# A streaming encoder step: PSUM reuse by tile, single banks in the down projection, frames split in two parts

## The chip, the core and the metric

The kernel runs on one core of one Trainium2 chip. The metric is device time in microseconds (us). TensorE (PE) does the matmuls and transposes and writes PSUM, which has eight banks of 128 x 512 floats; VectorE (DVE) and ScalarE (ACT) read PSUM and SBUF; GpSimd (POOL) adds in SBUF and issues some DMAs; SyncE (SP) and ACT issue the other DMAs.

## What is computed

One step of a one-layer encoder for 1152 rows (1024 prompt frames and 8 x 16 sample frames) of width 1024. The part that the change touches is the end of memory attention, the norm after it and the feed-forward block:

```python
def _rmsnorm(x, g):
    xf = x.astype(jnp.float32)
    y = xf * lax.rsqrt(jnp.mean(xf * xf, axis=-1, keepdims=True) + EPS)
    return (y * g.astype(jnp.float32)).astype(x.dtype)

def _swiglu(h, w_gate, w_up, w_down):          # hidden width 2816
    return (jax.nn.silu(h @ w_gate) * (h @ w_up)) @ w_down

x = x + _merge(a_out, sb_out, g_out_sgu[l], g_out_sb[l], w_out[l])     # gMLP group and stick-breaking attention
x = x + _mem_attend(_rmsnorm(x, ln_mem[l]), mk, mv, w_mq[l], w_mo[l])  # ends in o @ w_mo, the out-projection
x = x + _swiglu(_rmsnorm(x, ln_ffn[l]), w_ffn_gate[l], w_ffn_up[l], w_ffn_down[l])
y = _rmsnorm(x, ln_final)
```

## The kernel before

Every float32 product is made from three matmuls: each operand is split into a high part (a cast on ACT) and a low part (the rest, a subtraction on DVE; `split`, L126 and L127), and `mm3` (L130 to L132) multiplies high by high, high by low and low by high. The rows go in nine tiles of 128. Python writes the work in one order, and a scheduler that knows estimated costs sets the order of each engine's queue from it; at run time each queue is strictly in order, and an instruction waits on semaphores for what it reads and for the last users of the buffer that it writes.

The last 920 us have three stages.

**Out-projection, 881 to 997 us** (`out_in`, `out_mm`, `turn_halves`). For each row tile `out_in` loads and splits the attention output `oh`, `ol`; `out_mm` makes two halves of 512 columns in the two banks of one PSUM pair tile `pp` and DVE adds each to the residual `xt` (L1013), which goes to `x2_d` by a POOL DMA (L1014). `norm` squares and sums the row on ACT (L148), takes the inverse root on POOL (`inv_rms`, L141 and L142) and scales on DVE (L150) into `xs`. `turn_halves` of the tile before transposes `xs` by eight small matmuls (L1025), four into each bank of another pair, and makes the right-hand operands of the feed-forward block: splits into `b11`, `b21`, `b22`, and the differences `t1` (L1031, L1032), `t2` (L1035), `t3` (two operations, L1042, on DVE) and `t4` (two operations, L1044, on POOL).

**Gate and up products, 997 to 1503 us.** A two-by-two block scheme makes each block product from seven instead of eight: 22 units (11 groups of hidden columns for gate and up), seven products each, 24 matmuls of 128 x 288 columns per product (`multiply`, L1154). The left operands come from `left`: weights loaded as `raw`, four sums on POOL (L1078), a cast on ACT and a subtraction on DVE into a weight tile `wg`. Four buffers of the pool `wr` and one of `w2` serve in turn, so five weight tiles are in the ring, and `refill(4)` keeps four ready ahead. The right operands are `b11`, `b21`, `b22` and the split frames `c5` to `c4`, which `frames(n)` makes from `t1` to `t4` in four calls of `split`, 128 x 576 each. The first unit begins while the last row tile has not been transposed: `multiply(1)` and `multiply(2)` stand ahead of the last `turn_halves`. Products go out of PSUM by ACT copies and DVE or POOL additions (L1144) and by `hid_d`, a DRAM buffer.

**Down projection, 1503 to 1791 us.** The 22 hidden groups go in six chunks, the first of two groups, the others of four. `load` fetches a group's `hid_d` rows (`hr`) and down weights (`raw`) on SP's queue, `prep` splits them (`hid`, `wd`). For each chunk and row tile a pair of banks takes the two halves, and DVE adds each half into the residual `xr` (L1280). The `xr` tiles come back from `x2_d` by nine POOL DMAs at the stage's start (L1251). In the last chunk the final norm follows each tile.

Two things set what waits. A PSUM tile is one unit of the dependency tracking: a pair tile holds two banks, and a matmul into one of them waits for users of the tile. When a pool is closed and another takes its space, the new pool's tiles wait for the users of the old pool; with `reuse_waits="tile"`, which the SBUF pools have here already, a new tile waits only for the users of the tiles that lay under it, and without it for every user of the pool. The PSUM pools were without it.

Of the kernel before, what the change touches and what calls it, by code (L numbers as in the profile page):

```python
# [9 lines left out]
F32 = mybir.dt.float32  # L10
F32R = mybir.dt.float32r
# [5 lines left out]
P = 128  # L17
D = 1024
KC = D // P
NT = 9  # L20
# [17 lines left out]
def stream_step(ctx: ExitStack, tc: tile.TileContext, I, O, cst):  # L38
    nc = tc.nc

    def pool(stack, name, bufs=1, **kw):
        return stack.enter_context(tc.tile_pool(name=name, bufs=bufs, reuse_waits="tile", **kw))

    const = ctx.enter_context(tc.tile_pool(name="const", bufs=1))
    stP = ctx.enter_context(ExitStack())
    psum = [stP.enter_context(tc.tile_pool(name="psum", bufs=1, space=PSUM))]
    small = ctx.enter_context(tc.tile_pool(name="small", bufs=8))
    dram = ctx.enter_context(tc.tile_pool(name="scratch", bufs=1, space=DRAM))

# [3 lines left out]
    def nm(s):  # L53
        uid[0] += 1
        return f"{s}_{uid[0]}"
# [915 lines left out]

    with ExitStack() as stE:
        stP.close()
        psum[0] = stE.enter_context(tc.tile_pool(name="psum_pairs", bufs=1, space=PSUM))
        stN, stS, stG = ExitStack(), ExitStack(), ExitStack()
        slots = pool(stE, "f_h", bufs=10)

        def slot(shape, name):
            return slots.tile(shape, F32R, tag="h", name=name)
# [36 lines left out]
        def turn_halves(xs, i):  # L1016
# [16 lines left out]
            if n0 < P:  # L1033
                new = both[:, 1, :, n0:P]
                nc.vector.tensor_tensor(out=t2[:, :, c1], in0=new, in1=t1[:, :, c1], op=sub)  # L1035
                split(b22[0][:, :, c1], b22[1][:, :, c1], new)
                for out, b, eng in ((t3, b11, nc.vector), (t4, b21, nc.gpsimd)):
                    t = out[:, :, c1]
                    for m in range(2):
                        x, y = t if m else t2[:, :, c1], b[m][:, :, c1].bitcast(F32)  # L1040
                        if out is t3:
                            eng.tensor_tensor(out=t, in0=x, in1=y, op=sub)  # L1042
                        else:
                            eng.tensor_tensor(out=t, in0=y, in1=x, op=ALU.add if m else sub)  # L1044
# [9 lines left out]
        stW.close()  # L1054

        cp = pool(stG, "g_c", side="right")
        w2 = pool(stG, "g_w", bufs=1, side="right")
        sp = pool(stG, "g_s", side="right")
        vp = [pool(stG, "g_p", side="right")]
        right = {1: b11, 2: b21, 3: b22}  # L1060
# [5 lines left out]
        def left(w, f, order):  # L1066
# [13 lines left out]
            for n in order:  # L1080
                if n in (3, 5) and not s:
                    sum_(5, a21, a22, ALU.add)
                    sum_(6, s[5], a11, ALU.subtract)
                    sum_(7, a11, a21, ALU.subtract)
                    sum_(3, a12, s[6], ALU.subtract)
                src = {1: a11, 2: a12, 4: a22}.get(n, s.get(n))
                pl = wr if count[0] % 5 else w2
                count[0] += 1
                hl = pl.tile([P, 2, 4, P], F32R, tag="w", name=nm("wg"))
                split(hl[:, 0], hl[:, 1], src)  # L1090
                yield n, hl

        def frames(n):

            hi = cp.tile([P, 4, TH], F32R, name=f"c{n}h")
            lo = cp.tile([P, 4, TH], F32R, name="c5l") if n == 5 else slot([P, 4, TH], f"c{n}l")
            for c in range(4):
                split(hi[:, c], lo[:, c], {5: t1, 6: t2, 7: t3, 4: t4}[n][:, c])
            right[n] = hi, lo

        def bank_pair():
            n = count[1] % 4
# [59 lines left out]

        def load(f):

            hr = []
            for g in range(2):
                t = xp[0].tile([P, TH], F32, tag="x", name=nm("hr"))
                nc.sync.dma_start(t, hid_d[f, :, g * TH:(g + 1) * TH])
                hr.append(t)
# [17 lines left out]
        for u in range(len(units)):  # L1187
# [3 lines left out]
            end = u == len(units) - 1  # L1191
            for k, n in enumerate(order_of(u)):
                if u == 0 and k == 0:
                    refill(3)
                    part[1] = vt("p1", 2)
                    nc.scalar.copy(part[1], multiply(1))
                    part[2] = multiply(2)
                    turn_halves(norm(npool, ins[-1][1], gffn), NT - 1)
                    stN.close()
                    vp.append(pool(stG, "g_v", side="right"))  # L1200
                    xp.append(pool(stE, "g_x", bufs=6))
                    frames(5)
                    continue
                if u == 0 and k == 1:
                    continue
                refill(4)
                if u == 0 and n in (3, 5, 6):
                    frames({3: 6, 5: 7, 6: 4}[n])
                acc = multiply(n)
                if n in (1, 5):  # L1210
                    part[n] = vt(f"p{n}", 2 if n == 1 else 1)
# [30 lines left out]
                    have.append(prep(*loads[k - 4]))  # L1242
        stG.close()

        xpool = pool(stE, "h_x", side="right")
        jp = pool(stE, "h_j", bufs=2, side="right")
        gfin = xpool.tile([P, D], F32, name="gfin")
        xr = []
        for i in range(NT):
# [16 lines left out]
        for c, fs in enumerate(chunks):  # L1266
# [72 lines left out]
```

## Time and profile before

| | before |
|---|---|
| median of 3 runs | 1804.79 us (1803.49 to 1807.76) |
| the profiled execution | 1804.37 us, span 1801.5 us |
| PE busy | 1729.4 us (96%) |
| DVE busy | 980.3 us (54%) |
| ACT busy | 675.8 us (38%) |
| POOL busy | 445.5 us (25%) |
| mean granted TensorE clock | 0.983 of full speed |

The span is the time from the first to the last instruction on the chip; some 3 us lie around it. PE is the engine that sets the end: what matters is where it idles and where its clock is at half. In the rows below, "[4.76 <-DVE xs L150]" behind a PE instruction says that PE was idle for 4.76 us before it and that the end of DVE's instruction of line 150, which wrote `xs`, released it. Pitch is the distance from one matmul's start to the next one's.

### The profile page before, as it was taken

How to read it: one execution, taken by the hardware profiler on the slowest of the kernel's cores; microseconds unless marked ns; L12 is line 12 of the kernel's file. 1: busy time of each engine (PE TensorE's matmuls, PEld its weight loads, DVE VectorE, ACT ScalarE, POOL GpSimd, SP SyncE). 2: the span in 40 equal slices, each digit the busy share in tenths (PEclk: the TensorE clock that was granted, in tenths of full speed). 3: DMA queues.
4: the chain of work that ended last, by engine and by line, in shares of the span. 5: the costliest groups of instructions: out<-in, count | busy, mean ns of one | idle time of the engine just before them, and what ended most of it. 6: DMA issues, size and time to landing. Idle time of an engine off the chain costs nothing.

```text
span 1801.5 us, 26249 instructions
## 1 busy us (share of the span) xinstructions
PE 1729.4 (96%) x10039; PEld 1500.7 (83%) x10039; DVE 980.3 (54%) x1471; ACT 675.8 (38%) x1326; POOL 445.5 (25%) x582
## 2 busy tenths in 40 slices
PE   8999998999999999999799799999999998999997
PEld 6889886777777799898687699999999997777775
DVE  5322336888778745546446754455444456344444
ACT  5322134766555435546321432333222332011123
POOL 1101223444333210000013444444444431000002
PEclk9999999999999999999899899999999999999999
DMA  8457135467544524435543132222222227122202
GB/s 284 147 199 247 64 128 186 147 204 243 166 118 133 191 95 132 129 121 173 161 129 106 35 100 88 76 79 78 74 74 74 74 74 279 50 100 100 99 8 98
DMA packets 175069, 227.93 MB, mean 127 GB/s; under 512 B 12064, under 2 KB 122272, under 8 KB 174944
## 3 DMA queue, kind: packets, MB, share of 16 engines
q1 hardware_dynamic: 143248, 161.89, 29.4%
q10 hardware_dynamic: 23504, 35.79, 5.4%
q0 software_dynamic: 8192, 28.58, 4.3%
q8 instruction: 79, 1.29, 0.3%
q14 instruction: 46, 0.38, 0.1%
HBM read 161.86 MB, written 64.36 MB: 126 GB/s over the span
## 4 chain that ended last, share of the span: by engine, by line
PE 65%; DVE 4%; issue 2%; DMA 2%; POOL 2%; ACT 2%; POOLq 0%; ACTq 0%; SPq 0%; DVEq 0%
PE pp L1154 27%; PE pp L130 6%; PE pp L131 6%; PE pp L132 6%; PE acc L385 3%; PE acc L130 2%; PE acc L131 2%; PE acc L132 2%; PE z L385 2%; PE tr L389 2%; PE av L385 1%; DMA raw<-in_cache_mem_v_dram 1%; PE ov L943 1%; PE ss L926 1%; DMA or<-oT_d 1%
## 5 line engine op out<-in xcount | busy, mean ns | idle before, releaser
L1154 PE MATMUL pp<-b,wg 128*128 128x288 f32 x1584 | 224.1, 298 | 4.8 <-ACT b L126 3.4
L1154 PEld LDWEIGHTS pp<-b,wg 128*128 128x128 f32 x1584 | 216.1, 190 | 5.9 <-ACT b L126 3.8
L130 PE MATMUL pp<-wd,hid 128*128 128x512 f32 x396 | 153.7, 404 | 8.2 <-DVE xr L1280 6.6
L131 PE MATMUL pp<-wd,hid 128*128 128x512 f32 x396 | 155.3, 394 | 0.0
L132 PE MATMUL pp<-wd,hid 128*128 128x512 f32 x396 | 153.1, 392 | 0.0
L1280 DVE TENSOR_TENSOR xr<-pp,xr 128x512 f32<-128x512 f32 x108 | 73.4, 690 | 134.2 <-PE pp L132 132.8
L405 POOL TENSOR_TENSOR beta<-beta,pr 128x512 f32<-128x512 f32 (+4 forms) x104 | 95.4, 920 | 164.9 <-DVE pr L403 150.0
L130 PE MATMUL acc<-wh,hah 128*128 128x512 f32 x288 | 114.5, 397 | 2.7 <-ACT hah L126 2.7
L132 PE MATMUL acc<-wh,hal 128*128 128x512 f32 x288 | 113.9, 395 | 0.6 <-DVE hal L127 0.6
L131 PE MATMUL acc<-wl,hah 128*128 128x512 f32 x288 | 113.3, 393 | 0.0
L130 PEld LDWEIGHTS pp<-wd,hid 128*128 128x128 f32 x396 | 74.4, 189 | 35.6 <-DVE xr L1280 17.8
L126 ACT CAST wg<-s 128x512 fp32r<-128x512 f32 x88 | 54.3, 619 | 126.3 <-PE pp L1154 93.1
L126 ACT CAST hid<-hr 128x576 fp32r<-128x576 f32 x44 | 27.6, 671 | 195.3 <-PE pp L132 144.8
L127 DVE TENSOR_TENSOR wg<-s,wg 128x512 fp32r<-128x512 f32 x88 | 71.6, 817 | 50.1 <-ACT wg L126 49.0
L127 DVE TENSOR_TENSOR wg<-raw,wg 128x512 fp32r<-128x512 f32 x66 | 63.9, 968 | 46.6 <-ACT wg L126 46.4
L131 PEld LDWEIGHTS pp<-wd,hid 128*128 128x128 f32 x396 | 74.9, 189 | 15.7 <-DVE wd L127 1.1
L132 PEld LDWEIGHTS pp<-wd,hid 128*128 128x128 f32 x396 | 74.7, 189 | 15.8
L1014 POOL DMA_DIRECT2D x_d<-xt x9 | 5.7, 632 | 311.2 <-DVE xt L1013 311.2
L1292 POOL TENSOR_SCALAR sm<-sm 128x1 f32<-128x1 f32 x9 | 6.6, 737 | 270.8 <-ACT junk L1285 270.8
L126 ACT CAST wg<-raw 128x512 fp32r<-128x512 f32 x66 | 40.8, 619 | 87.3 <-issue 42.1
L385 PE MATMUL acc<-mw,aT 128*128 128x512 f32 x216 | 66.8, 421 | 0.1
L130 PEld LDWEIGHTS acc<-wh,hah 128*128 128x128 f32 x288 | 54.6, 190 | 13.5 <-ACT hah L126 2.9
(281 smaller groups left out, 4527.7 us busy)
## 6 DMA issues: line engine op xcount, KB each, us to landing
hid_d<-g ACTq DMA_DIRECT2D x44, 288.0 KB, 2.4
hr<-hid_d SPq DMA_DIRECT2D x44, 288.0 KB, 4.2
raw<-in_w_ffn_gate_dram SPq DMA_DIRECT2D x22, 512.0 KB, 3.8
raw<-in_w_ffn_up_dram SPq DMA_DIRECT2D x22, 512.0 KB, 3.9
raw<-in_w_ffn_down_dram SPq DMA_DIRECT2D x22, 512.0 KB, 4.9
raw<-in_w_in_dram SPq DMA_DIRECT2D x20, 512.0 KB, 5.1
x_d<-xt POOLq DMA_DIRECT2D x18, 512.0 KB, 3.1
raw<-in_cache_mem_k_dram SPq DMA_DIRECT2D x16, 512.0 KB, 4.2
```

The lines of the kernel that those rows point to most:

```text
L126: nc.scalar.copy(hi, src)
L127: nc.vector.tensor_tensor(out=lo, in0=src, in1=hi.bitcast(F32), op=ALU.subtract)
L130: nc.tensor.matmul(out, lhsT=lh, rhs=rh, start=first, stop=False)
L131: nc.tensor.matmul(out, lhsT=lh, rhs=rl, start=False, stop=False)
L132: nc.tensor.matmul(out, lhsT=ll, rhs=rh, start=False, stop=last)
L385: nc.tensor.matmul(out, lhsT=lhsT, rhs=rhs, start=start, stop=stop)
L389: nc.tensor.transpose(out, in_, idn)
L405: nc.gpsimd.tensor_tensor(out=beta[:, :w], in0=beta[:, :w], in1=pr[:, 1:w + 1], op=ALU.mult)
L926: nc.tensor.matmul(ss[:, g], lhsT=qm[:, dc, g, b4 * P:(b4 + 1) * P], rhs=flat(kt[n][:, dc]), start=b4 == 0 and dc == 0 and n == 0, stop=b4 ...
L943: nc.tensor.matmul(ov[:, g], lhsT=pm[:, n, g, b4 * P:(b4 + 1) * P], rhs=vv[m][:, n], start=b4 == 0 and n == 0 and m == 0, stop=b4 == 3 and ...
L1154: nc.tensor.matmul(acc[:, h], lhsT=hl[:, a, c], rhs=b[:, c, h * TN:(h + 1) * TN], start=c == 0 and k == 0, stop=c == 3 and k == 2)
L1280: nc.vector.tensor_tensor(out=xr[i][:, hs], in0=pd, in1=xr[i][:, hs], op=ALU.add)
```

## The change

- The PSUM pools are made with `reuse_waits="tile"`.
- In the down projection a pool of single banks, `tr` 0 to 7 in turn, takes the place of the pair tiles. It is a new pool; the pairs' pool is closed before it.
- `t4` moves from POOL to DVE.
- `frames` is called in two parts around the last `turn_halves`: the columns 0 to 448, which don't need the last row tile, before it for `c5` and `c6`, and the last 128 columns after it; `c7` and `c4` come after it in the same two parts. Each part goes in two calls over two of four column groups, 128 x 2 x 448 and 128 x 2 x 128, where before there were four calls of 128 x 576. `c6l` lies in the pool of the `c` tiles, not in a slot.
- The ring of weight tiles has four buffers, not five: `w2` is gone, and `refill(4)` becomes `refill(3)`.
- The first chunk's `hr` tiles lie in the slots' pool, so that the pool for later ones is opened only after the products' pools are closed.

```diff
-    psum = [stP.enter_context(tc.tile_pool(name="psum", bufs=1, space=PSUM))]
+    psum = [pool(stP, "psum", space=PSUM)]
...
-        psum[0] = stE.enter_context(tc.tile_pool(name="psum_pairs", bufs=1, space=PSUM))
+        stP = ExitStack()
+        psum[0] = pool(stP, "psum_pairs", space=PSUM)
...
-                for out, b, eng in ((t3, b11, nc.vector), (t4, b21, nc.gpsimd)):
+                for out, b, eng in ((t3, b11, nc.vector), (t4, b21, nc.vector)):
...
-        w2 = pool(stG, "g_w", bufs=1, side="right")
...
-                pl = wr if count[0] % 5 else w2
-                count[0] += 1
-                hl = pl.tile([P, 2, 4, P], F32R, tag="w", name=nm("wg"))
+                hl = wr.tile([P, 2, 4, P], F32R, tag="w", name=nm("wg"))
...
-        def frames(n):
+        CUT = (NT - 1) * P - TH
+        def frames(n, last):
...
-            for c in range(4):
-                split(hi[:, c], lo[:, c], {5: t1, 6: t2, 7: t3, 4: t4}[n][:, c])
+            t = {5: t1, 6: t2, 7: t3, 4: t4}[n]
+            for c in (slice(0, 2), slice(2, 4)):
+                ts = slice(CUT, TH) if last else slice(0, CUT)
+                split(hi[:, c, ts], lo[:, c, ts], t[:, c, ts])
...
-                    refill(3)
+                    refill(2)
...
-                    turn_halves(norm(npool, ins[-1][1], gffn), NT - 1)
+                    xs = norm(npool, ins[-1][1], gffn)
+                    frames(5, False)
+                    frames(6, False)
+                    turn_halves(xs, NT - 1)
                     stN.close()
                     vp.append(pool(stG, "g_v", side="right"))
-                    xp.append(pool(stE, "g_x", bufs=6))
-                    frames(5)
+                    frames(5, True)
...
-                refill(4)
+                refill(3)
...
+        stP.close()
+        psum[0] = pool(stE, "psum_end", space=PSUM)
+        banks(tr=range(8))
...
-                pp = pair((c * NT + i) % 4)
                 for half in range(2):
                     hs = slice(half * 512, (half + 1) * 512)
-                    pd = pp[:, half]
+                    pd = ps("tr", [P, 512])
```

The queues change in three places that matter here.

PE, the end of the out-projection before. `pp_9611` is the product of row tile 7, `pp_9688` that of row tile 8 (the last), `pp_9670` the transposes of row tile 6:

```order
L130 MATMUL pp_9688<-wh_8608,oh_9605 128x512
L131 MATMUL pp_9688<-wl_8609,oh_9605 128x512
L1025 MATMUL pp_9670<-csb,xs_9663 128x128 x4
L132 MATMUL pp_9688<-wh_8608,ol_9606 128x512
L130 MATMUL pp_9611<-wh_8608,oh_9517 128x512
L131 MATMUL pp_9611<-wl_8609,oh_9517 128x512
L132 MATMUL pp_9611<-wh_8608,ol_9518 128x512
```

The same place after:

```order
L130 MATMUL pp_9611<-wh_9010,oh_9517 128x512
L131 MATMUL pp_9611<-wl_9011,oh_9517 128x512
L132 MATMUL pp_9611<-wh_9010,ol_9518 128x512
L1026 MATMUL pp_9670<-csb,xs_9663 128x128 x4
L130 MATMUL pp_9688<-wh_8730,oh_9605 128x512
L131 MATMUL pp_9688<-wl_8731,oh_9605 128x512
L132 MATMUL pp_9688<-wh_8730,ol_9606 128x512
L130 MATMUL pp_9688<-wh_8736,oh_9605 128x512
L131 MATMUL pp_9688<-wl_8737,oh_9605 128x512
L1026 MATMUL pp_9670<-csb,xs_9663 128x128 x4
```

Before, the first four transposes of tile 6 stood two matmuls into tile 8, and tile 7's second half followed them; now both sets of four stand behind the whole of tile 7, the second of them five matmuls after the first.

POOL, from the last row tile's end to its norm, before. The `s` rows are sums of the first unit's weights, `t_8993` is `t4`, and the two `sm` rows at the end give the inverse root:

```order
L1078 TENSOR_TENSOR s_9789<-raw_9781 128x512
L1078 TENSOR_TENSOR s_9793<-raw_9779,raw_9781 128x512
L1078 TENSOR_TENSOR s_9791<-s_9789,raw_9779 128x512
L1014 DMA x_d<-xt_9603 128x1024
L1044 TENSOR_TENSOR t_8993<-b_8986,t_8991 128x4x128
L1078 TENSOR_TENSOR s_9795<-raw_9779,s_9791 128x512
L1044 TENSOR_TENSOR t_8993<-b_8987,t_8993 128x4x128
L141 TENSOR_SCALAR sm_9853<-sm_9853 128x1
L142 TENSOR_TENSOR sm_9855<-sm_9853,mhalf 128x1
```

The same place after:

```order
L1078 TENSOR_TENSOR s_9884<-raw_9778 128x512
L1078 TENSOR_TENSOR s_9888<-raw_9776,raw_9778 128x512
L1078 TENSOR_TENSOR s_9886<-s_9884,raw_9776 128x512
L1015 DMA x_d<-xt_9603 128x1024
L1078 TENSOR_TENSOR s_9890<-raw_9776,s_9886 128x512
L141 TENSOR_SCALAR sm_9839<-sm_9839 128x1
L142 TENSOR_TENSOR sm_9841<-sm_9839,mhalf 128x1
```

The two operations of `t4` are gone from between the row's sum and its inverse root; the four sums and the DMA still stand there.

DVE, the start of the down projection before. `xr_14941` and `xr_14943` are the residuals of row tiles 0 and 1, and `wd_15089` a group of down weights for the next chunk:

```order
L1280 TENSOR_TENSOR xr_14941<-pp_14966,xr_14941 128x512
L1280 TENSOR_TENSOR xr_14943<-pp_14981,xr_14943 128x512
L127 TENSOR_TENSOR wd_15089<-raw_15052,wd_15089 128x1024
L1280 TENSOR_TENSOR xr_14941<-pp_14966,xr_14941 128x512
L1280 TENSOR_TENSOR xr_14943<-pp_14981,xr_14943 128x512
L1280 TENSOR_TENSOR xr_14945<-pp_15010,xr_14945 128x512
L1280 TENSOR_TENSOR xr_14947<-pp_15025,xr_14947 128x512
```

The same place after, where `xr_14939` and `xr_14941` are row tiles 0 and 1:

```order
L127 TENSOR_TENSOR hid_14996<-hr_14958,hid_14996 128x576
L1293 TENSOR_TENSOR xr_14939<-tr_14964,xr_14939 128x512
L1293 TENSOR_TENSOR xr_14939<-tr_14972,xr_14939 128x512
L1293 TENSOR_TENSOR xr_14941<-tr_14980,xr_14941 128x512
L127 TENSOR_TENSOR hid_14996<-hr_14959,hid_14996 128x576
L1293 TENSOR_TENSOR xr_14941<-tr_14988,xr_14941 128x512
L127 TENSOR_TENSOR wd_15001<-raw_14962,wd_15001 128x1024
L1293 TENSOR_TENSOR xr_14943<-tr_15010,xr_14943 128x512
```

Before, the weights' subtraction stood behind the first half of two row tiles; now three halves of two row tiles are added before a second part of `hid`, the fourth follows, and then the weights.

## Rows read from the trace of the kernel before

**Rows 1.** Windows: us, then busy us and (instructions) by engine, PEclk, DMA, GB/s.

```profile
990.00:1030.00 40.00, 27.10 (x154) 24.35 (x155) 30.68 (x38) 17.35 (x31) 20.09 (x15) 0.79 0.12 40
...
1100.00:1300.00 200.00, 200.00 (x1515) 200.00 (x1514) 101.25 (x127) 59.40 (x98) 82.49 (x55) 1.00 0.25 79
...
1500.00:1550.00 50.00, 43.92 (x195) 35.20 (x194) 27.27 (x38) 7.64 (x10) 7.04 (x12) 0.97 0.59 217
```

**Rows 2.** Timeline of PE, start of the out-projection: start, length, instruction, idle before.

```profile
881.95 0.77 PE L130 MATMUL pp<-wh,oh 128*128 128x512 f32 x1 [0.61 <-DVE ot L953]
...
883.36 0.63 PE L130 MATMUL pp<-wh,oh 128*128 128x512 f32 x1
883.79 0.63 PE L131 MATMUL pp<-wl,oh 128*128 128x512 f32 x1
...
888.10 0.40 PE L130 MATMUL pp<-wh,oh 128*128 128x512 f32 x1
888.34 0.39 PE L131 MATMUL pp<-wl,oh 128*128 128x512 f32 x1
```

**Rows 3.** Timeline of PE, seven waits around the last transposes.

```profile
963.50 0.50 PE L130 MATMUL pp<-wh,oh 128*128 128x512 f32 x1 [0.75 <-DVE xt L1013]
...
977.07 0.63 PE L1025 MATMUL pp<-csb,xs 128*128 128x128 f32 x4 [1.81 <-DVE xs L150]
...
990.66 0.63 PE L1025 MATMUL pp<-csb,xs 128*128 128x128 f32 x4 [1.91 <-DVE xs L150]
...
1008.85 1.09 PE L1025 MATMUL pp<-csb,xs 128*128 128x128 f32 x4 [4.76 <-DVE xs L150]
...
1012.83 1.11 PE L1025 MATMUL pp<-csb,xs 128*128 128x128 f32 x4 [2.65 <-DVE t L1031]
1017.34 0.85 PE L1154 MATMUL pp<-b,wg 128*128 128x288 f32 x2 [3.39 <-ACT b L126]
1019.61 5.08 PE L1154 MATMUL pp<-b,wg 128*128 128x288 f32 x21 [1.43 <-DVE b L127]
```

**Rows 4.** Timeline of POOL, before the last norm.

```profile
997.04 1.51 POOL L1078 TENSOR_TENSOR s<-raw 128x512 f32<-128x512 f32 x1 [7.85 <-PE pp L132]
...
1002.70 1.30 POOL L1044 TENSOR_TENSOR t<-b,t 128x512 f32<-128x512 f32 x1
...
1005.16 1.27 POOL L1044 TENSOR_TENSOR t<-b,t 128x512 f32<-128x512 f32 x1
...
1006.81 0.57 POOL L142 TENSOR_TENSOR sm<-sm,mhalf 128x1 f32<-128x1 f32 x1
```

**Rows 5.** Timeline of DVE, around the last norm.

```profile
992.05 0.69 DVE L1032 TENSOR_TENSOR t<-t,b 128x512 f32<-128x512 f32 x1
...
999.12 1.79 DVE L1042 TENSOR_TENSOR t<-t,b 128x512 f32<-128x512 f32 x1
...
1007.41 1.28 DVE L150 SCALAR_TENSOR_TENSOR xs<-xt,sm,gffn 128x1024 f32<-128x1024 f32 x1 [4.79 <-POOL sm L142]
1008.62 3.56 DVE L127 TENSOR_TENSOR wg<-s,wg 128x512 fp32r<-128x512 f32 x4
...
1022.75 2.77 DVE L127 TENSOR_TENSOR c6l<-t,c6h 128x576 fp32r<-128x576 f32 x4
...
1031.58 0.75 DVE L1144 TENSOR_TENSOR u<-pp,p 128x576 f32<-128x576 f32 x1
```

**Rows 6.** Waits of ACT between 1040 and 1500: total us, times, longest.

```profile
ACT wg L126 <- PE pp L1154: 94.8, 40, 2.6
```

**Rows 7.** Timeline of PE, start of the down projection.

```profile
1518.24 0.50 PE L130 MATMUL pp<-wd,hid 128*128 128x512 f32 x1 [4.46 <-DVE xr L1280]
```

**Rows 8.** Timeline of DVE, start of the down projection.

```profile
1516.36 1.23 DVE L127 TENSOR_TENSOR wd<-raw,wd 128x1024 fp32r<-128x1024 f32 x1 [5.23 <-ACT wd L126]
```

**Rows 9.** Timeline of PE, two waits in the last chunk.

```profile
1759.62 0.50 PE L130 MATMUL pp<-wd,hid 128*128 128x512 f32 x1 [0.81 <-DVE xr L1280]
...
1788.34 0.50 PE L130 MATMUL pp<-wd,hid 128*128 128x512 f32 x1 [1.28 <-DVE xr L1280]
```

More of the change, by code (lines that the diff above doesn't have):

```diff
@@ L1086, in left @@
                 src = {1: a11, 2: a12, 4: a22}.get(n, s.get(n))
-                pl = wr if count[0] % 5 else w2
-                count[0] += 1
-                hl = pl.tile([P, 2, 4, P], F32R, tag="w", name=nm("wg"))
+                hl = wr.tile([P, 2, 4, P], F32R, tag="w", name=nm("wg"))
                 split(hl[:, 0], hl[:, 1], src)
                 yield n, hl
-        def frames(n):
-            hi = cp.tile([P, 4, TH], F32R, name=f"c{n}h")
-            lo = cp.tile([P, 4, TH], F32R, name="c5l") if n == 5 else slot([P, 4, TH], f"c{n}l")
-            for c in range(4):
-                split(hi[:, c], lo[:, c], {5: t1, 6: t2, 7: t3, 4: t4}[n][:, c])
-            right[n] = hi, lo
+        CUT = (NT - 1) * P - TH
+        def frames(n, last):
+            if n not in right:
+                hi = cp.tile([P, 4, TH], F32R, name=f"c{n}h")
+                lo = cp.tile([P, 4, TH], F32R, name=f"c{n}l") if n in (5, 6) else slot([P, 4, TH], f"c{n}l")
+                right[n] = hi, lo
+            hi, lo = right[n]
+            t = {5: t1, 6: t2, 7: t3, 4: t4}[n]
+            for c in (slice(0, 2), slice(2, 4)):
+                ts = slice(CUT, TH) if last else slice(0, CUT)
+                split(hi[:, c, ts], lo[:, c, ts], t[:, c, ts])
         def bank_pair():
@@ L1163, in load @@
         def load(f):
-            hr = []
+            if xp:
+                hr = [xp[0].tile([P, TH], F32, tag="x", name=nm("hr")) for _ in range(2)]
+            else:
+                both = slots.tile([P, 2, TH], F32, tag="h", name=nm("hr"))
+                hr = [both[:, g] for g in range(2)]
             for g in range(2):
-                t = xp[0].tile([P, TH], F32, tag="x", name=nm("hr"))
-                nc.sync.dma_start(t, hid_d[f, :, g * TH:(g + 1) * TH])
-                hr.append(t)
+                nc.sync.dma_start(hr[g], hid_d[f, :, g * TH:(g + 1) * TH])
             raw = rawp.tile([P, D], F32, tag="raw", name=nm("raw"))
@@ L1205, in stream_step @@
                     continue
-                refill(4)
+                refill(3)
                 if u == 0 and n in (3, 5, 6):
-                    frames({3: 6, 5: 7, 6: 4}[n])
+                    for part_ in (False, True):
+                        if n != 3 or part_:
+                            frames({3: 6, 5: 7, 6: 4}[n], part_)
                 acc = multiply(n)
@@ L1243, in stream_step @@
         stG.close()
+        stP.close()
+        psum[0] = pool(stE, "psum_end", space=PSUM)
+        banks(tr=range(8))
         xpool = pool(stE, "h_x", side="right")
         jp = pool(stE, "h_j", bufs=2, side="right")
+        xp.append(pool(stE, "h_h", bufs=6, side="right"))
         gfin = xpool.tile([P, D], F32, name="gfin")
```

## The prediction

> **What bounds the kernel now.** I read the windows first, from the out-projection on. In the units of gate and up PE is busy for all of its time at full clock: 200.00 of 200 us [rows 1]. There a change can only lose. Two windows are different: between 990 and 1030 us PE works 27.10 of 40 us at 0.79 of its clock, and between 1500 and 1550 us 43.92 of 50 us at 0.97. DVE and POOL stay under 31 of the 40 us in the first of them, so no engine is full there; PE waits for chains of small operations. Then I read PE's timeline in these stretches for every start with an idle time in its brackets. The reader is to see eleven of them: one at the start of the out-projection [rows 2], seven around the last transposes, 0.75 + 1.81 + 1.91 + 4.76 + 2.65 + 3.39 + 1.43 = 16.70 us [rows 3], one at the start of the down projection, 4.46 us [rows 7], and two in its last chunk, 0.81 + 1.28 us [rows 9]. Last I read what DVE and POOL did ahead of the release of each [rows 4, 5, 8]: there it shows whether the change takes out the reason of a wait or only moves it. PE waits 23.9 us in all at these eleven places, and this is what the change can get at.
>
> **The out-projection's start.** The first matmul waited 0.61 us for DVE's `ot`, the last user of the old PSUM pool, which has nothing to do with the bank that it writes [rows 2]. With waits by tile it needs only the users of its own two banks, long done. That takes 0.6 us off, if `ot`'s reader is not under these banks; at worst 0. The clock may give more: the pitch is 0.43 us at 883.36 and 0.24 at 888.34, so the stretch from 881.95 to 888.10, 6.2 us, would be 3.4 us at full clock. Without the idle time the clock could rise earlier, at best by those 2.8 us. But PE has been waiting off and on before this stretch too, for work that doesn't change, so I take 0.6, with bounds of 0 and 3.4.
>
> **The end of the out-projection.** PE's rows show the transposes of tile 6 moved from two matmuls into tile 8 to behind all of tile 7. That is later by a half of 24 matmuls of 0.24 us [rows 2], 5.8 us, so the norm is there in time: the 1.81 and the 1.91 us go. In exchange tile 8's second half, which waited 0.75 us for DVE's addition of the first half in the same pair, will wait longer. PE has 18 matmuls of 0.24 us and a set of transposes left in front of it, some 4.7 us. DVE has to do an addition, eight operations of `turn_halves` (two of them are `t4`'s, new on DVE) and then the addition that is waited for: ten operations over 512 columns, some 0.62 us each (four over 576 take 2.77 us [rows 5]), so 6.2 us. A new wait of 1.5 us, and up to 2.7 if each operation that needs the one before it starts 0.15 us late, an estimate. Before there were 4.47 us of waits, after 1.5 to 2.7: a gain of 1.8 to 3.0, I take 2.
>
> **The last norm.** PE waited 4.76 us for `xs` [rows 3], DVE 4.79 us of idle time for POOL's inverse root [rows 5], and POOL's queue ahead of it holds four sums, a DMA and `t4`'s two operations, 1.30 and 1.27 us, from 997.04 to 1007.38 us [rows 4]. Without these two it ends 2.6 us earlier. But DVE has now ten operations to do between the end of the last matmul and `xs`, 1.2 us more than before in the plain reading, and those with two operands in SBUF are slow while POOL works: 1.79 us against 0.69 us alone [rows 5]. With four sums in POOL's queue, up to four of ten cost 1.1 us more. Both queues start at the end of the last matmul, 997.0 us [rows 4]: 997.0 + 6.2 + 4.4 = 1007.6 us at worst, 1003.2 at best, and POOL's end at 1004.8. So `xs` comes between 2.6 us earlier and 0.2 us later; I take the middle, rounded: 1.3 us earlier.
>
> The Trainium skill, page "SBUF — State Buffer", section "Who interferes with whom", says why: a VectorE instruction with two SBUF inputs and a GpSimd instruction that reads SBUF share an interface, and whoever is first keeps it for a whole instruction. The trace agrees with 1.79 against 0.69 us. By that rule an operation that leaves POOL frees its DVE neighbour, so `t4` on DVE would cost nothing in the tiles before, since `t3` gets back as much; by the plain count it costs 1.2 us per tile. The sum would be some 1 us larger by the rule alone; I keep the plain count.
>
> Behind it, before L1031's pair of operations, DVE now has four low parts of `c5` and `c6` over 128 x 2 x 448. Four parts of 128 x 576 took 2.77 us [rows 5]; by elements, 3584 against 2304, these take some 4.2 us. Before, four subtractions of `wg` stood there, 3.56 us for the four [rows 5]. So the wait of 2.65 us becomes some 3.3. The next two, 3.39 and 1.43 us, get shorter: POOL's sums no longer run beside these operations, which gives back 1.1 us on each of two, and the rest of `c5` is a quarter of the columns: 2.2 and 0.4. One is added. The subtractions of `c7` and `c4` and `t4`'s operations stand ahead of the addition `u` (1031.58 us [rows 5]), and in the new order PE needs `u`'s bank 4 matmuls after the product that `u` reads, where before another whole product of 24 lay between, 3.2 us (200 us x 24 / 1515 matmuls [rows 1]). The wait is 0 to 3.2 us; with `c7` and `c4` ahead, twice 2.77 us of work [rows 5], I take 2.0, nearer to the upper end. All five: 12.2 before (4.76 + 2.65 + 3.39 + 1.43), 3.5 + 3.3 + 2.2 + 0.4 + 2.0 = 11.4 after. The low clock of the window goes with the waits: 0.21 of 40 us is 8.4 us of lost work [rows 1], of which the last norm's waits hold the most; I take back 0.8, a tenth, bounds 0 and 3. The whole end, from 960 to 1033 us: 2 + 0.8 + 0.8 = 3.6 us faster, bounds 4 slower (each of DVE's moved operations at 1.7 us) and 7 faster.
>
> **The start of the down projection.** PE waited 4.46 us for an addition of DVE [rows 7]. DVE's queue says why: it stood for 5.23 us before the subtraction of a weight tile at 1516.36 us, whose cast on ACT, and so its load, was late [rows 8], with the additions behind it; all banks were full by then, since with pairs a bank is free only when its partner is. After the change PE has eight banks of its own, and DVE adds four halves ahead of the weights. Each half of this chunk is six matmuls, 1.4 us. With four added and eight banks full PE can be 12 halves in while DVE stands, 17 us after the stage's start at 1503, which is 1520; the weights were there at 1516.4. So the 4.46 us go. The clock was at 0.97 in this window, 50 x 0.03 = 1.5 us of lost work [rows 1]; I lay that to the wait, and it goes with it. The first matmuls into a bank that the last product used wait as before. Together 6.0 us, bounds 0 and 7.
>
> **The last chunk.** The two waits of 0.81 and 1.28 us [rows 9] are for the addition of the first half, while the second bank of the pair is free. With single banks they go: 2.1 us, bounds 0 and 2.1. The work behind the last matmul stays as it is.
>
> The Trainium skill, page "PSUM — Partial Sum Buffer", section "PSUM bank collisions raise a hardware error", asks to guard PSUM by bank and quadrant. By that a matmul into the second bank needs no wait for an addition that reads the first. The rows show that it waits here, 0.81 and 1.28 us; so the waits come from how the pair is tracked, and single banks end them.
>
> **The ring of weight tiles.** Four buffers instead of five cost nothing as long as a tile is made in time. ACT waits for PE to free a buffer, 94.8 us in 40 times [rows 6]: the ring is full, and the next tile is cast when a product ends. It is needed four products later with five buffers, 12.7 us, and three with four, 9.5 us. Per product of 3.2 us ACT is busy for 0.9 us and DVE for 1.6 (59.40 and 101.25 of 200 us [rows 1]), so a tile that goes through both is made in some 2.5 us, and 9.5 covers that. I take 0.
>
> **Sum.** 0.6 + 3.6 + 6.0 + 2.1 = 12.3 us. The profiled execution took 1804.4 us (its span of 1801.5 and some 3 around it, which stay), so 1792.1; the median lies 0.4 us above it: 1792.5. Adding the bounds, from 4 us slower to 20 faster, would take all at their ends at once, which is unlikely.
>
> **Rivals.** First, slower: the ring of four starves PE. 22 units have 154 products in 480 us, and any delay there is paid at once, since PE has no idle time [rows 1]. It decides once a tile takes more than 9.5 us from the free buffer to its last subtraction. One microsecond in each unit would be 22, less the 12.3 gained: 1814.5 us. Against it speaks that ACT waits on PE, and not the other way round, 40 times, 2.6 us at the longest [rows 6]. Chance 0.04.
>
> Second, DVE is too full around the last norm: +4 instead of -3.6 there, for 1800 us. For it speak 30.68 of 40 us [rows 1] and 1.79 us per operation beside POOL [rows 5]; against it, that POOL has less to do there. Chance 0.13.
>
> Third, the gain at the down projection's start is eaten by its loads: the first chunk's successors are now fetched behind the down weights on SP's queue while nine residual tiles come in (a load already held DVE for 5.23 us there [rows 8]), and DVE's queue has `hid` and `wd` between the additions. Then nothing of the 6.0 us is left: 1798.5. Chance 0.1.
>
> Fourth, the clock gives more, because the waits that go are those that sent it to half: 2.8 us at the out-projection and 3 at the last norm: 1786.7. Chance 0.12. The forecast itself has 0.61, between 1788 and 1797.
>
> **Range and chances.** From 1786 to 1800 us: the second rival lies at its upper edge, the first outside. A change of 0.2% (3.6 us) can just be told from none here. Faster by more than that is everything under 1801.2: 0.90. Within it: 0.06, from the second and third rivals together. Slower: 0.04.
>
> **What would show it.** In the changed kernel's timeline of PE: no idle time before the first out-projection matmul; no waits for `xs` but one, of 2 to 4 us; one wait of 1 to 3 us for `xt` in the last row tile; a new wait for `u` of about 2 us; in the down projection no wait for `xr` and a window from 1500 to 1550 us with full clock behind its first 3 us; and 1100 to 1300 us still 200 of 200 us. The forecast is wrong if PE idles in the units, if `xs` comes no earlier behind the last matmul than 10 us, or if a wait for `hid` or `wd` stands at the first chunk's end.

## The result and the profile after

The changed kernel takes 1779.31 us (median of 4 runs, 1778.3 to 1781.57) against 1805.2 us before in the same comparison: a ratio of 0.9857, with an interval of 0.984 to 0.9874, so 25.9 us faster. I had forecast 1792.5 us and 1786 to 1800. The direction was right, the size was half of what came, and the range did not hold it.

The profiled execution has a span of 1776.5 us, 25.0 less than before. The starts of PE's matmuls cut both spans into the same stages:

| stretch (us) | before | after | change |
|---|---|---|---|
| to the last transposes (L951) ahead of the out-projection | 880.7 | 879.5 | -1.2 |
| from there to its first matmul | 1.26 | 0.40 | -0.9 |
| out-projection, to the first product | 115.3 | 110.9 | -4.4 |
| products, to the first matmul of the down projection | 506.3 | 504.9 | -1.4 |
| down projection, to its last matmul | 287.4 | 270.3 | -17.1 |
| behind it | 10.5 | 10.5 | 0.0 |

The first row holds nothing of the change: in all the profiles of this study the last L951 starts within a band of 4.7 us, in no order that follows the edits. The down projection holds two thirds of the gain. By chunks (one of two groups, five of four) it took 33.11, 50.59, 50.38, 50.36, 50.31 and 52.69 us before, and 24.61, 49.13, 49.20, 49.20, 49.20 and 48.97 after.

PE's timeline after, all starts with an idle time from the end of the out-projection on (start, length, instruction, idle before):

```profile
960.36 0.50 PE L130 MATMUL pp<-wh,oh 128*128 128x512 f32 x1 [0.41 <-DVE xt L1014]
984.87 0.50 PE L130 MATMUL pp<-wh,oh 128*128 128x512 f32 x1 [1.57 <-DVE xt L1014]
...
1001.39 0.63 PE L1026 MATMUL pp<-csb,xs 128*128 128x128 f32 x4 [3.46 <-DVE xs L150]
...
1005.91 1.12 PE L1026 MATMUL pp<-csb,xs 128*128 128x128 f32 x4 [3.62 <-DVE t L1032]
1008.93 0.85 PE L1158 MATMUL pp<-b,wg 128*128 128x288 f32 x2 [1.90 <-ACT b L126]
...
1010.54 4.24 PE L1158 MATMUL pp<-b,wg 128*128 128x288 f32 x21 [0.28 <-DVE b L127]
...
1021.69 0.50 PE L1158 MATMUL pp<-c5h,wg 128*128 128x288 f32 x2 [0.41 <-DVE u L1148]
...
1495.72 0.50 PE L130 MATMUL tr<-wd,hid 128*128 128x512 f32 x1 [0.85 <-DVE t L1148]
```

Against [rows 3] the two waits for `xs` within the out-projection are gone, and the second half of the last row tile has a new wait of 1.57 us for `xt`, as forecast. The 0.75 us of before is not the wait that it replaces: at 963.50 us it stands two row tiles earlier, and 0.41 us are left of it. The last norm's four waits were 12.2 us and are five of 9.7. The waits of [rows 7, 9] are gone. The down projection had one bracket more before, which is not among the eleven of the prediction:

```profile
1506.46 0.50 PE L130 MATMUL pp<-wd,hid 128*128 128x512 f32 x1 [1.62 <-DVE t L1144]
```

It waits for the bank of a late product, and the 0.85 us in the last row of PE's timeline after are what is left of it, now ahead of the stage. But all these terms don't add up to 17 us in the down projection. The rest is in a place that I had not looked at: the windows of its steady part, of before and of after (columns as in [rows 1]),

```profile
1540.00:1700.00 160.00, 160.00 (x688) 126.75 (x688) 71.98 (x98) 27.65 (x39) 0.00 (x0) 1.00 0.26 91
```

```profile
1515.00:1675.00 160.00, 160.00 (x704) 131.34 (x703) 73.27 (x101) 29.71 (x42) 0.00 (x0) 1.00 0.27 95
```

say that PE was busy for 160.00 of 160 us both times, at full clock, and did 688 matmuls in the one and 704 in the other. A busy PE is not PE at its peak. What held it is in the waits of PEld, the weight loads, over the whole down projection; first before (releaser, total us, times, longest us):

```profile
PEld pp L130 <- DVE xr L1280: 17.8, 37, 4.9
PEld pp L130 <- DVE t L1144: 2.0, 1, 2.0
PEld pp L131 <- DVE wd L127: 1.1, 5, 0.3
PEld pp L130 <- ACT wd L126: 1.1, 5, 0.3
```

and then after:

```profile
PEld tr L131 <- DVE wd L127: 1.5, 5, 0.3
PEld tr L130 <- DVE t L1148: 1.1, 1, 1.1
```

Weight loads waited 37 times for an addition, and PE's own brackets showed three of these. One of the other 34, before, on PE and then on PEld:

```profile
1607.23 0.76 PE L130 MATMUL pp<-wd,hid 128*128 128x512 f32 x2
1607.84 0.39 PE L131 MATMUL pp<-wd,hid 128*128 128x512 f32 x1
1608.07 0.40 PE L132 MATMUL pp<-wd,hid 128*128 128x512 f32 x1
```

```profile
1607.01 0.19 PEld L130 LDWEIGHTS pp<-wd,hid 128*128 128x128 f32 x1
1607.50 0.19 PEld L130 LDWEIGHTS pp<-wd,hid 128*128 128x128 f32 x1 [0.30 <-DVE xr L1280]
1607.61 0.19 PEld L131 LDWEIGHTS pp<-wd,hid 128*128 128x128 f32 x1
```

The two matmuls of L130 take 0.61 us to the next start, where two take 0.45 elsewhere. The second one's weights were loaded 0.30 us late, when DVE had added the pair's other half. PE has no bracket there: its matmuls are 0.39 us long at a pitch of 0.23, so one that starts 0.16 us late still starts before the last one's modelled end.

### The profile page after: what moved, and what is told of

It reads as the page before. It is cut to its first block, busy times and chain, and to the rows that moved or that the text cites. A ratio compares the mean times of both kernels' runs of the same rounds, so it can differ in the third digit from the quotient of the medians.

```text
span 1776.5 us, 26280 instructions
## 1 busy us (share of the span) xinstructions
PE 1718.3 (97%) x10039; PEld 1501.5 (85%) x10039; DVE 987.3 (56%) x1481; ACT 678.2 (38%) x1326; POOL 435.4 (25%) x572
## 4 chain that ended last, share of the span: by engine, by line
PE 65%; DVE 4%; DMA 2%; issue 2%; ACT 2%; POOL 1%; SPq 0%; POOLq 0%; ACTq 0%; DVEq 0%
PE pp L1158 27%; PE tr L131 5%; PE tr L130 5%; PE tr L132 5%; PE acc L385 3%; PE acc L130 2%; PE acc L131 2%; PE acc L132 2%; PE pp L130 2%; PE z L385 2%; PE pp L131 2%; PE pp L132 2%; PE tr L389 2%; PE av L385 1%; PE ov L943 1%
## 5 line engine op out<-in xcount | busy, mean ns | idle before, releaser
L131 PE MATMUL tr<-wd,hid 128*128 128x512 f32 x396 | 154.6, 391 | 0.0
L132 PE MATMUL tr<-wd,hid 128*128 128x512 f32 x396 | 154.1, 389 | 0.0
L130 PE MATMUL tr<-wd,hid 128*128 128x512 f32 x396 | 151.5, 389 | 0.9 <-DVE t L1148 0.9
L127 DVE TENSOR_TENSOR wg<-s,wg 128x512 fp32r<-128x512 f32 x88 | 87.7, 996 | 103.4 <-ACT wg L126 102.5
L1293 DVE TENSOR_TENSOR xr<-tr,xr 128x512 f32<-128x512 f32 x108 | 73.3, 689 | 121.0 <-PE tr L132 117.6
L130 PE MATMUL acc<-wh,hah 128*128 128x512 f32 x288 | 114.5, 398 | 2.6 <-ACT hah L126 2.6
L130 PEld LDWEIGHTS tr<-wd,hid 128*128 128x128 f32 x396 | 74.4, 188 | 17.0 <-DVE t L1148 1.1
L131 PEld LDWEIGHTS tr<-wd,hid 128*128 128x128 f32 x396 | 74.3, 188 | 16.7 <-DVE wd L127 1.5
L132 PEld LDWEIGHTS tr<-wd,hid 128*128 128x128 f32 x396 | 74.4, 188 | 15.3
L1078 POOL TENSOR_TENSOR s<-raw 128x512 f32<-128x512 f32 x22 | 28.9, 1315 | 156.0 <-DMA raw<-in_w_ffn_up_dram 75.4
L127 DVE TENSOR_TENSOR wl<-raw,wh 128x1024 fp32r<-128x1024 f32 x36 | 43.7, 1221 | 41.0 <-ACT wh L126 40.4
```

Of the source, the lines that this page charges most:

```text
L127: nc.vector.tensor_tensor(out=lo, in0=src, in1=hi.bitcast(F32), op=ALU.subtract)
L130: nc.tensor.matmul(out, lhsT=lh, rhs=rh, start=first, stop=False)
L131: nc.tensor.matmul(out, lhsT=lh, rhs=rl, start=False, stop=False)
L132: nc.tensor.matmul(out, lhsT=ll, rhs=rh, start=False, stop=last)
L1078: nc.gpsimd.tensor_tensor(out=s[n], in0=x, in1=y, op=op)
```

## The experiments

The first question was where the 17.1 us of the down projection come from. Theory 1: a pair tile makes a half wait for its partner's addition, everywhere and mostly below PE's brackets. Theory 2: only my four terms.

**Single banks alone.** Before, with the down projection's banks of after:

```diff
-        psum[0] = stE.enter_context(tc.tile_pool(name="psum_pairs", bufs=1, space=PSUM))
+        stP = ExitStack()
+        psum[0] = stP.enter_context(tc.tile_pool(name="psum_pairs", bufs=1, space=PSUM))
...
+        stP.close()
+        psum[0] = pool(stE, "psum_end", space=PSUM)
+        banks(tr=range(8))
...
-                pp = pair((c * NT + i) % 4)
...
-                    pd = pp[:, half]
+                    pd = ps("tr", [P, 512])
```

> Before, with single banks in the down projection alone. Theory 1 (a pair tile makes its second half wait for the addition of its first, in each of the row tiles, mostly for 0.1 to 0.3 us that show only in the idle time of the weight loads): the down projection goes from 287.8 to some 271 us, the whole to 1787 to 1789 us. Theory 2 (the gain there is my four terms alone: 4.46 + 1.5 + 0.81 + 1.28 = 8.1 us, and the rest of the 25 us lies ahead of it): 1797 us.

1790.42 us, ratio 0.9924 (0.9908 to 0.9941): 13.8 us. The chunks take 27.40, 49.19, 49.26, 49.22, 49.19 and 48.99 us, all but the first as after, and no weight load waits for an addition. The down projection gains 14.2 us, but its first matmul now waits 2.76 us for the last product's bank, ahead of it (before, 1.62 us within the stage). Theory 2 falls; theory 1's total was 1.4 us too low, with that wait and a first chunk of 27.40 us where after has 24.61.

**Pairs again.** After, with the pair tiles:

```diff
-        stP.close()
-        psum[0] = pool(stE, "psum_end", space=PSUM)
-        banks(tr=range(8))
...
+                pp = pair((c * NT + i) % 4)
...
-                    pd = ps("tr", [P, 512])
+                    pd = pp[:, half]
```

> After, with pair tiles in the down projection again. Theory 1: the down projection is back at 285 to 288 us with weight loads waiting for the addition some 37 times: 1794 to 1797 us. Theory 2: only 8 us come back: 1787 us.

1788.77 us, ratio 0.9916 (0.9902 to 0.9931), 9.5 us more than after (10.6 by the two ratios). The waits of the weight loads are back:

```profile
PEld pp L130 <- DVE xr L1290: 14.4, 34, 2.0
```

The steady chunks are at 50.2 to 50.5 us again and the last one at 52.63. But the first is at 26.59 us, not 33.1: of the stall of 4.46 us only 1.59 us come back with the pairs. Neither theory had that.

**Pairs, with alternating halves.** Is it the wait for the partner, or that four pairs are fewer than eight banks? Before, with the order of the halves changed: first halves of two row tiles, then their second halves. The final norm has a third scratch buffer for it.

```diff
-        jp = pool(stE, "h_j", bufs=2, side="right")
+        jp = pool(stE, "h_j", bufs=3, side="right")
...
-            for i in range(NT):
+            seq = [(i + k, h) for i in range(0, NT - 1, 2) for h in range(2) for k in range(2)] + [(NT - 1, 0), (NT - 1, 1)]
...
+            for i, half in seq:
```

> Before, pair tiles kept in the down projection, but the halves of two row tiles alternate (first halves of both, then second halves of both), so that the addition of a half is over before its partner starts. Theory 1 (it is the wait for the partner that costs): the steady chunks run at 0.227 us per matmul as after, and all but the stall at the stage's start goes: some 9 us, 1794 to 1796 us. Rival (it is the number of banks, four pairs against eight singles, that costs): no gain in the steady chunks, 1803 to 1806 us.

1801.24 us, ratio 0.9989 (0.998 to 0.9999). The four steady chunks take 197.5 us instead of 201.6 (after: 196.7), and the waits in them, here from 1540 to 1740 us in before and then in this kernel,

```profile
PEld pp L130 <- DVE xr L1280: 7.5, 25, 0.3
```

```profile
PEld pp L130 <- DVE xr L1284: 1.2, 4, 0.3
```

are nearly gone. So it is the wait for the partner's addition, with the same four pairs. The total gains 2.9 us, less than theory 1 said, since the last chunk is 2.0 us longer, where theory 1 had it shorter: a second half now waits 2.71 us for an addition that stands behind the final norm's operations on DVE.

The second question was the first chunk.

**The ring of four, and the ring with the loads.** Before, with four weight tiles; then also with the first chunk's `hr` in the slots and the later ones' pool opened behind the products, pairs kept:

```diff
-        w2 = pool(stG, "g_w", bufs=1, side="right")
...
-                pl = wr if count[0] % 5 else w2
...
+                both = slots.tile([P, 2, TH], F32, tag="h", name=nm("hr"))
...
-                    xp.append(pool(stE, "g_x", bufs=6))
...
+        xp.append(pool(stE, "h_h", bufs=6, side="right"))
```

> Before, with four weight tiles in the ring instead of five (w2 gone, one product less ready ahead). The prediction's term is 0: 1803 to 1805 us, and PE busy for all of 1100 to 1300 us. Rival 1 of the prediction: PE waits for wg in the units, 1 us or more in each of 22: 1815 us or more.

> As the ring of four, and the hid rows of the first chunk lie in the slots, their pool for later chunks opened after the products' pools, as in after; pair tiles everywhere. Theory (the stall of 4.46 us at the down projection's start came from a load that stood behind others, and the new place of hr sends the down weights ahead): the first chunk takes 26 to 28 us instead of 33.1, the steady chunks stay at 50.3 us: 1797 to 1799 us. Rival (the stall is the pairs'): 33 us, 1803 to 1805 us.

The ring alone: 1804.65 us, ratio 1.0004 (0.9994 to 1.0014), PE busy for 200.00 of 200 us between 1100 and 1300; the term of 0 was right within the interval of 1.1 us faster to 2.5 slower, and the first rival is out. With the loads: 1799.06 us, ratio 0.997 (0.9959 to 0.9982), and a first chunk of 26.60 us with pairs, 6.5 less, while the products are 2.4 us longer. The issues of SP's queue in before, and then in this kernel, show why:

```profile
1495.96 0.33 SPq L1171 DMA_DIRECT2D raw<-in_w_ffn_down_dram  x1
1499.03 2.23 SPq L1168 DMA_DIRECT2D hr<-hid_d  x2
1505.77 0.33 SPq L1171 DMA_DIRECT2D raw<-in_w_ffn_down_dram  x1
```

```profile
1494.06 4.67 SPq L1170 DMA_DIRECT2D raw<-in_w_ffn_down_dram  x3
1498.78 9.33 SPq L1168 DMA_DIRECT2D hr<-hid_d  x6
```

The weights for which DVE stood at 1516.36 us [rows 8] were issued at 1505.77, while the nine loads of the residual went out (POOL issues them from 1503.75 on); now three groups of weights are issued ahead of all of those. PE keeps one wait in this chunk, which ends with an addition that stood 2.33 us for a residual tile:

```profile
1516.33 0.50 PE L130 MATMUL pp<-wd,hid 128*128 128x512 f32 x1 [1.63 <-DVE xr L1279]
```

So there are two ways out of this stall, and the change has both: with single banks PE has room to go on, with the loads DVE doesn't stand for the weights. The banks take out the whole of it, the loads all but 1.6 us. In after DVE stands 3.11 us for a residual tile at 1502.68 us, and PE has no bracket there.

**Down weights issued early, nothing else.** The same idea by a smaller edit: the next chunk's `raw` tiles issued first.

```diff
+            return hr, early.pop(f) if f in early else down(f)
...
+                    early.update({f: down(f) for f in chunks[1][:3]})
```

> Before, with pair tiles, where the down weights of the next chunk's first three groups are issued ahead of their hid rows and of the residual's loads; DVE's order is the same. Theory (the 4.46 us stall at the stage's start is a late load that DVE's queue waits for): the stall goes with pairs too, the first chunk takes 27 to 28 us instead of 33.1: 1798 to 1800 us. Rival (the banks are the cause): 33 us as before, 1804 us.

1803.16 us, ratio 0.9996 (0.9984 to 1.0008), first chunk 33.53 us. The edit did not move the load: `raw` has three buffers, and the late tile was still issued at 1505.34 us, when a buffer came free. It tells nothing on the cause.

The third question was the stretch ahead of the down projection, 6.7 us.

**Waits by tile alone.** Before, with both PSUM pools' waits by tile (the edit of the second):

```diff
-        psum[0] = stE.enter_context(tc.tile_pool(name="psum_pairs", bufs=1, space=PSUM))
+        psum[0] = pool(stE, "psum_pairs", space=PSUM)
```

> Before, with the PSUM pools' waits by tile and nothing else. The first out-projection matmul no longer waits for the last user of the old pool. The prediction's term: 0.6 us (0 to 3.4), so 1801.8 to 1804.6 us. Rival: since the clock is half there, PE's earlier start gives 2 us or more: 1802.5 or less, with fewer than 10 matmuls at half clock.

1803.16 us, ratio 0.9991 (0.9982 to 1.0): 0 to 3.2 us. The step from the last L951 to the first matmul is 0.61 us instead of 1.26, the out-projection 115.1 instead of 115.3 us. The term was about right; the clock gives little: some eleven matmuls still run at half clock, where the rival had fewer than ten. Its 2 us lie within the interval.

**`t4` on DVE alone, and back on POOL in after.**

```diff
-                for out, b, eng in ((t3, b11, nc.vector), (t4, b21, nc.gpsimd)):
+                for out, b, eng in ((t3, b11, nc.vector), (t4, b21, nc.vector)):
```

> Before, with t4 on DVE and nothing else. Theory 1 (POOL's queue holds the last norm back by t4's two operations): the last wait for xs falls from 4.8 us by 1 to 2.6 us and the next ones get no longer: 1801 to 1803 us. Rival (DVE is the engine that is full there): the wait for xs falls by less than 0.5 us or the waits behind it grow by as much: 1804 to 1806 us.

> After, with t4 back on POOL. Theory 1: of the 4.4 us that the way from the first out-projection matmul to the first product became shorter nothing depends on t4 (it is the new order of the transposes), and the wait for xs in the last turn grows from 3.5 to 4.8 us: 1780 to 1782 us. Rival: the order follows from t4's place, since the scheduler counts its cost, and all of it goes back: 1784 to 1786 us.

On DVE alone: 1800.06 us, ratio 0.9976 (0.9964 to 0.9988), and the out-projection takes 111.9 us instead of 115.3, a gain that neither theory had. Back on POOL in after: 1787.09 us, ratio 0.99 (0.9877 to 0.9923), 7.8 us more than after, the out-projection at 115.3 us and the products at 508.8 instead of 504.9. Its timeline of PE has the old waits again, and a longer one for the last `xs`:

```profile
975.13 0.63 PE L1026 MATMUL pp<-csb,xs 128*128 128x128 f32 x4 [1.82 <-DVE xs L150]
988.71 0.63 PE L1026 MATMUL pp<-csb,xs 128*128 128x128 f32 x4 [1.91 <-DVE xs L150]
...
1007.62 1.09 PE L1026 MATMUL pp<-csb,xs 128*128 128x128 f32 x4 [5.80 <-DVE xs L150]
```

So the place of the transposes follows from `t4`'s engine, through the scheduler: the rival's reason held there, though the total came out 1 us above its range, since the products grew too. In the kernel with `t4` on DVE alone the last wait for `xs` is 2.54 us, 2.2 less, and the one for ACT's `b` behind it is 4.42 us instead of 3.39: the last turn as a whole stays at 506.3 us.

**Frames late.** After, with the first parts of `c5` and `c6` behind the last transposes:

```diff
-                    frames(5, False)
-                    frames(6, False)
                     turn_halves(xs, NT - 1)
...
+                    frames(5, False)
                     frames(5, True)
```

> After, with the first parts of c5 and c6 behind the last transposes, where the last parts are. Theory (those four subtractions, 4 us on DVE, only change places: the wait ahead of the second set of transposes, 3.6 us, falls to under 1, and the products of c5 and c6 wait for as much): 1778 to 1781 us. Rival (the split takes DVE's work out of the last turn): 1782 us or more, with a wait for c5 or c6 of over 2 us.

1779.62 us, ratio 0.9866 (0.9852 to 0.9881), the same as after. The wait in front of the second set of transposes is 0.81 instead of 3.62 us, the one for `b` 2.60 instead of 1.90, and one of 1.63 us for `wg` came ahead of `c5`'s product. The theory held: the order of the split isn't worth anything by itself.

**Three edits together.** Before, with single banks, waits by tile and `t4` on DVE:

```diff
+        psum[0] = pool(stP, "psum_pairs", space=PSUM)
...
+                for out, b, eng in ((t3, b11, nc.vector), (t4, b21, nc.vector)):
...
+                    pd = ps("tr", [P, 512])
```

> Before, with single banks in the down projection, waits by tile in the PSUM pools and t4 on DVE, but the frames whole, five weight tiles and the loads as before. If the parts add up (measured alone: 13.8, 1.0 and 3.7 us): 1785 to 1787 us. Rival (frames and loads add nothing): 1779 us, as after.

1784.24 us, ratio 0.9895 (0.9878 to 0.9912): 19.9 us, where the parts make 18.5 by themselves. So the parts about add up, and the rival falls. Most of what after has beyond that is in the products (504.9 against 508.7 us, 1.9 of it the wait ahead of the down projection, 0.85 against 2.76) and the first chunk (24.61 against 26.25), so in the ring, frames and loads together. The frames' split has no run of its own. The first 400 matmuls of the products, which hold the last norm, took 70.6 us before, 70.1 here, 72.4 with ring and loads alone, 71.5 in after with `t4` back on POOL, and 67.5 in after. No run has this gain without both `t4` on DVE and the split frames; the runs that have it have the ring and the loads too, so what the split gives by itself is not shown.

**Single banks in the out-projection too.** What the rest suggests for after: `out_mm` and `turn_halves` with banks of their own.

```diff
-        psum[0] = pool(stP, "psum_pairs", space=PSUM)
+        psum[0] = pool(stP, "psum_out", space=PSUM)
+        banks(oo=range(4), tt=range(4, 8))
...
-                pa = acc[:, half]
+                pa = ps("oo", [P, 512])
```

> After, with single banks in the out-projection and its transposes too (a pool of its own, closed before the products; the last transposes stay in a pair). Theory 1 (a pair's second half waits for the addition of its first): the waits for xt, 0.41 and 1.57 us, and some eight short ones in the weight loads there go: 2 to 3.5 us less, 1776 to 1777.5 us. Rival (PE has no work to fill in, it waits for xs instead): 1778.5 to 1780 us.

1780.52 us, ratio 0.9864 (0.9841 to 0.9888), no better than after: theory 1 falls. The out-projection is 1.9 us shorter (109.0 us) and the waits for `xt` are gone, but the products are 3.4 us longer: the new order has a matmul of `c6` early, which waits for a weight tile. The rival's time is nearly right but not its wait: the one for `xs` fell to 0.96 us.

```profile
1004.92 0.61 PE L1165 MATMUL pp<-c6h,wg 128*128 128x288 f32 x1 [5.62 <-ACT wg L126]
```

## Why the prediction was right in direction and wrong in size

- **What bounds the kernel.** This is the step that failed: "PE waits 23.9 us in all at these eleven places, and this is what the change can get at." I took PE's brackets and its busy share for all of its lost time. The pairs also cost some 0.17 us in most row tiles, in weight loads that waited 0.30 us. The four steady chunks became 4.9 us shorter (201.6 to 196.7), which my sum had at nothing; alternating halves take away 4.2 of it with the pairs kept, so that much is the wait for the partner. The rule of the Trainium skill that I had weighed (page "PSUM — Partial Sum Buffer", section "PSUM bank collisions raise a hardware error") asks for a guard by bank and quadrant, which needs no wait for an addition in the partner bank. The runs agree with it: with single banks none of the 37 waits of weight loads for an addition is left. I had looked for such waits only at the two places where PE showed one.
- **The last chunk**: 2.1 us forecast, 3.7 measured. The two waits went, with the restart behind each 2.65 us; five short ones of the same kind are some 0.9 more.
- **The start of the down projection**: 6.0 us forecast, 8.5 measured, or 7.65 less the wait of 0.85 us that now stands ahead of the first matmul. The 4.46 us went, and with them the clock's 1.5: nine matmuls behind the stall, from 1519.04 to 1522.67 us, took 3.63 us instead of some 2.04, and the granted clock is 1.00 in the whole chunk after, 0.95 before. What I had missed is the bracket of 1.62 us at 1506.46, which I had left standing as a wait for a bank of the last product; the last 0.8 us stay open. The reason that I gave for the stall is one of two: with the loads of after most of it goes with pairs too. The load of the weights, on which I built the third rival, was a gain, not a loss.
- **The out-projection's start**: 0.6 us forecast, 0.9 in the profiles, 0 to 3.2 in the runs with this part alone.
- **The end of the out-projection**: waits of 4.47 us became 1.98, a gain of 2.5, where I took 2. I had laid the 0.75 us to the wrong tile: what the forecast calls a longer wait is a new one of 1.57 us, and the old one shrank to 0.41, so that this term came near is in part luck. The stage lost 4.4 us in all; 0.4 of it is a set of transposes that now stands behind the first product, and 1.0 the start, whose first 15 matmuls take 5.1 us instead of 6.15, since the clock rises after some nine of them instead of thirteen. The last 0.5 us stay open.
- **The last norm**: I had 11.4 us of waits after, there are 9.67. `xs` starts 9.5 us behind the first sum (999.97 and 990.51 us) against 10.4 before, so 0.9 earlier where I took 1.3. POOL's queue is done by 998.98 us, 8.5 behind its first sum where I had 7.8, and DVE is the later of the two:

```profile
992.83 1.79 DVE L1033 TENSOR_TENSOR t<-t,b 128x512 f32<-128x512 f32 x1
...
996.25 1.99 DVE L1045 TENSOR_TENSOR t<-b,t 128x512 f32<-128x512 f32 x1
...
999.37 0.68 DVE L1045 TENSOR_TENSOR t<-b,t 128x512 f32<-128x512 f32 x1
999.97 1.27 DVE L150 SCALAR_TENSOR_TENSOR xs<-xt,sm,gffn 128x1024 f32<-128x1024 f32 x1
```

  Two of DVE's operations are slow beside POOL's sums (1.79 and 1.99 us), not four. The waits for `u` (0.41 us where I took 2.0) and for `b` came out shorter, the one for L1032 a little longer. The clock's 0.8 us came too: the first 400 matmuls of the stage take 67.5 us instead of 70.6, 3.1 less, with 2.6 us less of waits and 0.4 us more of transposes, so some 0.9 is left for the clock. In the stage's first 40 us the granted clock is 0.87 instead of 0.79, and the 21 matmuls behind the last wait for `b` take 4.24 us instead of 5.08. The stage as a whole lost only 1.4 us, since the wait ahead of the down projection costs 1.0 in it and the units became 0.6 us longer.
- **The ring**: 0 forecast, and 0 within the interval for the ring alone. But the units of after are slower, with PE busy for all of its time, where [rows 1] has 1515 matmuls:

```profile
1100.00:1300.00 200.00, 200.00 (x1513) 200.00 (x1512) 104.42 (x124) 62.01 (x101) 80.96 (x54) 1.00 0.24 74
```

  From the 401st matmul of the products to the last it is 435.6 us before, 435.8 with the ring of four, and 436.2 with the loads too and in after. It is 0.6 us, and its cause stays open.

12.3 us were forecast, and the profiles differ by 23.8 behind the first row of the table. Of the 11.5 missing, 9.0 are in the down projection (17.1 against 8.1) and 2.5 ahead of it. The 9.0 are 4.9 in the steady chunks, 1.6 in the last one and 2.5 in the first. None of the rivals was near: the fourth, 1786.7 us, came closest, but it was built on the clock, which gave 1.0 us at the out-projection's start and some 0.9 at the last norm, where it had 2.8 and 3.

## What to carry to other kernels

Where PE is 100% busy, count matmuls per window against the best pitch that the kernel reaches anywhere, and read the idle time of the weight loads: short waits on semaphores hide there, and a tracked tile that is larger than what one group writes can make one at each group (here in some 26 of the 36 row tiles of the steady chunks). An edit that moves an operation to another engine can be worth more through the order that the scheduler makes of it than through the operation; test it alone, since two edits may remove the same stall, and a term found with one of them is not there for the other.

## What was not expected of the hardware

A weight load that came 0.30 us late cost the matmul behind it some 0.16 us, since loads run ahead of the matmuls that use them (by 0.22 us in the rows above, 1607.01 and 1607.23 us), and left PE's busy time whole. Some thirty such waits took about 5.3 us from the steady chunks and the last one, more than the 4.46 us of the largest stall that PE showed, though that stall cost some 1.6 us more by the clock behind it.
